# Padding the SBUF pools of a decoder layer so that what TensorE reads starts at multiples of 256 bytes

## The chip, the cores and the metric

One core of a Trainium2 chip runs one program. The metric is the device time of one execution in microseconds, less is better. Engines: TensorE (PE in the profile, its weight loads apart as PEld), VectorE (DVE), ScalarE (ACT), GpSimd (POOL) and SyncE (SP, which issues most DMAs). SBUF is the on-chip memory that all of them read; a tile takes the same bytes in each of 128 partitions. TensorE writes to PSUM.

## What is computed

A decoder layer on 512 tokens of 1,024 features, float32 in and out:

```python
h = rmsnorm(x, g_mix);  proj = h @ w_in
# a gated DeltaNet group (conv, l2norm, chunked delta rule) and a sparse-attention group
# (indexer, top-k of 128 keys, softmax with a position bias)
x = x + concat([o_dn, o_dsa]) @ w_out
qx = rmsnorm(x, g_xattn) @ w_xq;  kvx = rmsnorm(mem, g_mem) @ w_xkv   # 256 memory tokens
x = x + softmax_attention(qx, kvx) @ w_xo
hf = rmsnorm(x, g_ffn)
x = x + (silu(hf @ w_gate) * (hf @ w_up)) @ w_down                    # 2816 wide
return rmsnorm(x, g_final)
```

## The kernel before

Activations lie feature-major: a tile [128 features, 512 tokens] for each 128 features. For precision at speed, each large product is made of three: a float32 operand is split into a high part, rounded to float32r (the type that TensorE reads in one pass), and the low rest, also float32r. `split` (lines 128 to 130) does it, with a copy on ScalarE and a subtraction on VectorE, and `mm3` (lines 136 to 139) issues the three matmuls, the weights' part first and the activations' second in the call: the first is stationary, the second moving. In the profile's names the moving tile comes first: `ps<-XH,wh` streams XH over the stationary wh.

```python
def mm3(o, lh, ll, rh, rl, start, stop):
    pe.matmul(o, lh, rh, start=start, stop=False)
    pe.matmul(o, lh, rl, start=False, stop=False)
    pe.matmul(o, ll, rh, start=False, stop=stop)
```

`weights` (lines 143 to 157) loads 512 KB into wraw (one of three buffers, issued by SP), and splits it into wh and wl (two buffers each). `dense` (line 159) makes 8 times three matmuls of 512 columns with it. That is how the projections of the head (`project`), the output projections (`project_out`), the queries of the cross attention and the gate, up and down projections of the FFN (`gated`, line 1021, and the loop behind it) work. The keys of the cross attention have 256 columns. The values (lines 937 to 939), the gates of the DeltaNet group (496 to 498) and the last part of the down projection (1061 to 1063) are token-major: there the weights are moving and the activations stationary. The very last of these use wz, one large split tile, for 48 matmuls. At the start, x is multiplied with the 464 columns of w_in of the sparse-attention group (lines 280 to 282), from tiles wd, wdh and wdl of [128, 2, 464]. A few products are plain float32: the DeltaNet's own, the logits of half of the sparse heads, and the transposes, which multiply by an identity out of cst.

The order of each engine's instructions comes from the program's order and from a scheduler that the framework runs when the kernel is built. Where a tile lies is decided by pools: const, wp (weights) and tmp from the left end of the free part of SBUF, others behind them, and the pools called "right" from the right end downwards. A pool packs its tiles one behind the other, at multiples of 32 bytes. The free part begins at byte 16,512 and ends at 229,344. The const pool holds many small tiles (`small`, line 216: columns of statistics, 4 to 128 bytes), so what stands behind it begins wherever their sum ends.

Of the kernel before, what the change touches and what calls it, by code (L numbers as in the profile page):

```python
# [16 lines left out]
T = 512  # L17
# [10 lines left out]
# pairs of DSA heads whose logits are products over 128 partitions  # L28
# [3 lines left out]
_CONST_COLS = 6 * 128  # L32
# [33 lines left out]
def laid_out(a):  # L66
    """Inputs as the launch takes them: x feature-major, vectors gathered by partition or into one row."""
    par = []
    for name in PAR:
        v = np.asarray(a[name])  # L70
        par.append(np.tile(v.reshape(1, 64), (1, 2)) if name.startswith("kidx") else v.reshape(-1, 128))
    rows = [np.asarray(a[name]).reshape(-1) for name in ROW]
    r = {name: np.ascontiguousarray(a[name]) for name in _INS}
    r["xT"] = np.ascontiguousarray(np.asarray(a["x"])[0].T)
    r["w_ukT"] = np.ascontiguousarray(np.asarray(a["w_uk"])[0].transpose(2, 0, 1)).reshape(128, 512)
    r["w_uvT"] = np.ascontiguousarray(np.asarray(a["w_uv"])[0].transpose(1, 0, 2)).reshape(128, 512)
    r["params"] = np.ascontiguousarray(np.concatenate(par).T)
    r["rows"] = np.ascontiguousarray(np.concatenate(rows)).reshape(1, N_ROW)
    return r
# [3 lines left out]
def hybrid_block(ctx, tc, I, out):  # L83
# [3 lines left out]
    const = ctx.enter_context(tc.tile_pool(name="const", bufs=1))  # L87
    wp = ctx.enter_context(tc.tile_pool(name="wp", bufs=1))
# [77 lines left out]
    # ---------------------------------------------------------------- constants and parameters  # L166
# [15 lines left out]
    warm = const.tile([128, 128], FT, name="warm")  # L182
# [5 lines left out]
    prT = const.tile([128, N_PAR], FT, name="prT")  # L188
    act.dma_start(prT, I["params"])
    w_in = I["w_in"][0]  # L190
    wd = [xload.tile([128, 2, N_DSA], FT, name=f"wd{j}") for j in range(4)]
# [9 lines left out]
    cst = const.tile([128, 6, 128], FT, name="cst")  # L201
    ident, tri, ones = cst[:, 0, :], cst[:, 1, :], cst[:, 5, :]
    sp.dma_start(cst, I["consts"].rearrange("p (k c) -> p k c", c=128))
    brow = const.tile([128, N_ROW], FT, name="brow")
# [6 lines left out]
    mhalf = const.tile([128, 16], FT, name="mhalf")  # L211
# [4 lines left out]
    def small(n, dt=FT):  # L216
        n_small[0] += 1
        return const.tile([128, n], dt, name=f"sm{n_small[0]}")
# [6 lines left out]
    def row_of(cols):  # L225
        """[128 tokens, 4 tiles] -> [128, 512] with the same row on every partition."""
        q = ps()
        for t in range(NT):
            pe.matmul(q[:, t * 128:(t + 1) * 128], cols[:, t:t + 1].to_broadcast([128, 128]), ident,
                      start=True, stop=True)  # L230
        o = const.tile([128, T], FT, name=f"row{n_small[0]}", tag="row", bufs=1)
        act.activation(o, q, AF.Copy)
        return o

    class Stats:
        """Sum of squares of feature-major tiles, per token."""
# [21 lines left out]
    # ---------------------------------------------------------------- x, and the DSA columns token-major  # L258
# [3 lines left out]
    wdh, wdl = ([xload.tile([128, 2, N_DSA], FR, name=f"wd{x}{j}") for j in range(4)] for x in "hl")  # L262
# [31 lines left out]
    # norms of the small projections, and their transposes  # L294
# [43 lines left out]
    # ---------------------------------------------------------------- GDN projections of one head, feature-major  # L338
# [33 lines left out]
    # ---------------------------------------------------------------- indexer scores  # L372
# [4 lines left out]
    for pr_ in range(4):  # L377
        q = ps()
        ms = slice(pr_ * 128, (pr_ + 1) * 128)
        for k in range(2):  # L380
            mm3(q, wq[:, 0, k, ms], wq[:, 1, k, ms], cqh[k], cql[k], k == 0, k == 1)
        # [high part; low part] of a head's queries on 128 partitions meets the keys' high part in one product
        st = qst[pr_]
        ql = cv(dt=FR)
        for s, r in enumerate(HALF):
            act.activation(st[s][r], q[r], AF.Copy)
            dve.tensor_tensor(ql[r], q[r], f32(st[s][r]), op=OP.subtract)
            sp.dma_start(f32(st[s][HALF[1 - s]]), f32(ql[r]))
# [30 lines left out]
    # ---------------------------------------------------------------- decay and beta, columns (head, chunk)  # L419
# [24 lines left out]
    # decay between the tokens of a chunk, and from its start  # L444
# [14 lines left out]
    # ---------------------------------------------------------------- relative position bias  # L459
    rb = const.tile([32, 8], FT, name="rb")  # L460
# [5 lines left out]
    # minus the bias, so that a row's minimum is minus the maximum of its logits, and from the far bucket's on:  # L466
    # a softmax is the same for logits that are all moved by one number
# [7 lines left out]
    def topk():  # L475
        m8 = dsa.tile([128, 8], FT, name="m8")
        for it in range(16):
            for t in (3, 2, 1):
                dve.max(m8, score[t])  # L479
                dve.match_replace(score[t], m8, score[t], MARK)  # L480
            yield
        for t in (1, 2, 3):
            dve.tensor_scalar(score[t], score[t], MARK, -NEG, op0=OP.not_equal, op1=OP.mult)
        yield
# [25 lines left out]
    def latents():  # L510
        """Queries and keys of the DSA heads, in pairs; values token-major."""
        u = [gdn.tile([128, 512], FT, name=n, tag=f"zg{i}") for i, n in enumerate(("w_ukT", "w_uvT"))]
        sp.dma_start(u[0], I["w_ukT"])
        sp.dma_start(u[1], I["w_uvT"])
        for pr_ in range(4):
            ms = slice(pr_ * 128, (pr_ + 1) * 128)
            q = ps("mm")
            for k in range(2):
                mm3(q, wu[:, 0, k, ms], wu[:, 1, k, ms], cqh[k], cql[k], k == 0, k == 1)
            qd.append(dsa.tile([128, T], FT, name=f"qd{pr_}", tag=f"od{pr_}"))  # L520
            act.activation(qd[pr_], q, AF.Copy, scale=-0.125)
            q = ps("mm")
            pe.matmul(q, u[0][:, ms], ckvT, start=True, stop=True)
            kT.append(dsa.tile([128, T], FT, name=f"kT{pr_}", tag=f"ol{pr_}"))
            act.activation(kT[pr_], q, AF.Copy)
        for t in range(NT):
            q = ps("mm")
            pe.matmul(q, ckvT[:, t * 128:(t + 1) * 128], u[1], start=True, stop=True)
            vt.append(dsa.tile([128, 512], FT, name=f"vt{t}"))
            act.activation(vt[t], q, AF.Copy)  # L530

    # ---------------------------------------------------------------- DSA attention
    OD = []

    def attention():
# [5 lines left out]
        for pr_ in range(4):  # L541
# [8 lines left out]
            if pr_ in STACKED:  # L550
                # per head, [high part; low part] of the queries on 128 partitions, and the keys' high part twice
# [10 lines left out]
            for t in range(NT):  # L562
# [9 lines left out]
                for s in range(2):  # L572
# [16 lines left out]
                    # block (keys kb, queries t) at column 384 kb + 128 t  # L589
# [16 lines left out]
    # ---------------------------------------------------------------- gated delta rule  # L606
# [58 lines left out]
    def diagonal_blocks():  # L665
        """Inverse of the 16 x 16 diagonal blocks, one per partition."""
# [10 lines left out]
        # 4 x 4 blocks by substitution, then twice the size: X21 = X22 (- N21) X11  # L677
# [27 lines left out]
    def level(lev):  # L705
        """Inverse of twice the block size: X -= X C X, with C the blocks below the diagonal."""
# [17 lines left out]
    def last_level():  # L724
        """The same for the one pair of blocks that is left, rows 64: and columns :64 of C."""
# [20 lines left out]
    def recurrence():  # L746
        # q scale: sigma = 128^-1/2 (|q|^2 + eps)^-1/2
# [12 lines left out]
        for c in range(NT):  # L760
# [9 lines left out]
            if c:  # L770
                q = ps("g")
                heads(q, lambda h: (QK[h][:, 0, cs], S[:, h, :]))
                # one accumulation group for the four heads: only its first product clears the bank
# [80 lines left out]
    # ---------------------------------------------------------------- residual stream, feature-major  # L854
# [25 lines left out]
    # memory, normalised and feature-major  # L880
# [25 lines left out]
    # first the heads that are done first  # L906
# [4 lines left out]
    # ---------------------------------------------------------------- cross attention  # L911
# [31 lines left out]
    def probs(h):  # L943
        a_, b_ = (xa.tile([128, 2, T], FR, name=f"px{x}{h}", tag=f"px{x}", bufs=2) for x in "hl")
        PX[h] = a_, b_
        for t2 in range(2):
# [7 lines left out]
            c4 = tmp.tile([128, 8], FT, name=f"x4_{h}_{t2}", tag="x4", bufs=4)  # L954
# [58 lines left out]
    # ---------------------------------------------------------------- SwiGLU  # L1013
# [31 lines left out]
    # the last columns, with the residual stream and the rest of the layer token-major  # L1045
# [9 lines left out]
    for hf in range(2):  # L1055
# [14 lines left out]
        if hf:  # L1070
            # the last pieces as one, so that the tiles are done one after another
            raw, wh, wl = (ff.tile([128, 4, 512], d_, name=f"wz{i}") for i, d_ in enumerate((FT, FR, FR)))
            sp.dma_start(raw, I["w_down"][0, 18 * 128:, cols].rearrange("(k p) c -> p k c", p=128))
            split(wh, wl, raw)
            for t in range(NT):
                for k in range(4):
                    part(t, wh, wl, k, 2 + k)
# [17 lines left out]
    banks["pool"].release()  # L1095

# [19 lines left out]
```

## Time and profile before

| | |
|---|---|
| median of 3 runs | 875.5 us (872.02 to 876.1) |
| span of the profiled execution | 875.0 us |
| TensorE busy | 846.8 us (97%) |
| VectorE, ScalarE, GpSimd busy | 501.9, 368.1, 207.8 us |
| DMA | 87.00 MB, mean 99 GB/s |

The span runs from the first to the last instruction of one profiled execution; of that execution no other time is known, and the three runs beside it are other executions. Busy time of TensorE is the union of its matmuls, which overlap in a pipeline: the next one starts while the one before is still draining. What a matmul costs is therefore the distance between starts, not its duration.

### The profile page before, as it was taken

The page shows a single profiled execution, that of the slowest core. Times are in us where ns is not written, and L with a number is a line of the kernel's source. Part 1 is how long each engine was busy: PE and PEld are TensorE (multiplying, and loading weights), DVE is VectorE, ACT ScalarE, POOL GpSimd, SP SyncE. Part 2 cuts the span into 40 slices and gives each one's busy share as a digit, 9 for nine tenths or more (in the row PEclk, how much of TensorE's full clock was granted, in tenths as well). Part 3 has the DMA queues.
Part 4 walks back from the last instruction along what each step waited for, and adds up shares of the span by engine and source line. Part 5 has one row for each costly group of instructions (what it writes and reads, how often), then busy time and mean ns, then how long its engine had stood idle before and what let it go on. Part 6 is the DMA issues. An engine that isn't in the chain of part 4 may idle for free.

```text
span 875.0 us, 10849 instructions
## 1 busy us (share of the span) xinstructions
PE 846.8 (97%) x4058; PEld 680.2 (78%) x4058; DVE 501.9 (57%) x873; ACT 368.1 (42%) x723; POOL 207.8 (24%) x213
## 2 busy tenths in 40 slices
PE   9999969789999999999999999999999999999996
PEld 7876847678767889888887888888888888888885
DVE  8786759989777564464455444453344443345542
ACT  6573846435666543353434432221133222233332
POOL 5546835546321122000003221110011110001112
PEclk9998979999999999999999999999999999999999
DMA  8541355244022434243323533233333333323302
GB/s 282 144 101 47 42 124 137 66 109 97 19 55 84 158 97 145 81 137 101 97 67 98 167 97 97 84 90 106 88 90 96 97 97 97 96 81 88 97 24 97
DMA packets 136652, 87.00 MB, mean 99 GB/s; under 512 B 9688, under 2 KB 125592, under 8 KB 136600
## 3 DMA queue, kind: packets, MB, share of 16 engines
q1 hardware_dynamic: 135736, 84.69, 34.1%
q10 hardware_dynamic: 864, 1.62, 0.5%
q8 instruction: 32, 0.52, 0.2%
q14 instruction: 20, 0.16, 0.1%
HBM read 77.10 MB, written 7.09 MB: 96 GB/s over the span
## 4 chain that ended last, share of the span: by engine, by line
PE 82%; DMA 6%; DVE 6%; issue 2%; ACT 2%; POOL 1%; SPq 0%; POOLq 0%; ACTq 0%; DVEq 0%
PE ps L137 21%; PE ps L139 21%; PE ps L138 21%; DMA tb_d<-t2k 4%; PE ps L597 1%; PE ps L568 1%; PE ps L588 1%; PE ps L398 1%; PE ps L396 1%; PE ps L1061 1%; PE ps L1063 1%; PE ps L1062 1%; PE ps L766 1%; PE ps L937 1%; PE ps L939 1%
## 5 line engine op out<-in xcount | busy, mean ns | idle before, releaser
L129 ACT ACTIVATE wh<-wraw 128x1024 fp32r<-128x1024 f32 x120 | 127.2, 1061 | 319.6 <-PE ps L138 179.0
L137 PE MATMUL ps<-XH,wh 128*128 128x512 f32 x512 | 204.3, 399 | 0.0
L139 PE MATMUL ps<-XH,wl 128*128 128x512 f32 x512 | 203.7, 398 | 0.0
L138 PE MATMUL ps<-XL,wh 128*128 128x512 f32 x512 | 203.1, 397 | 0.0
L130 DVE TENSOR_TENSOR wl<-wraw,wh 128x1024 fp32r<-128x1024 f32 x108 | 153.7, 1424 | 67.6 <-ACT wh L129 67.2
L137 PEld LDWEIGHTS ps<-XH,wh 128*128 128x128 f32 x512 | 96.9, 189 | 22.6 <-ACT Dm L454 0.6
L138 PEld LDWEIGHTS ps<-XL,wh 128*128 128x128 f32 x512 | 96.8, 189 | 22.0 <-issue 0.2
L139 PEld LDWEIGHTS ps<-XH,wl 128*128 128x128 f32 x512 | 96.9, 189 | 21.6
L1032 POOL TENSOR_TENSOR t2k<-t2k,t2k 128x512 f32<-128x512 f32 x22 | 30.6, 1390 | 297.4 <-DVE t2k L1031 249.7
L247 POOL TENSOR_TENSOR acc<-acc,t2k 128x512 f32<-128x512 f32 x21 | 36.0, 1715 | 179.4 <-ACT t2k L246 179.1
L1031 DVE TENSOR_TENSOR t2k<-ps,row 128x512 f32<-128x512 f32 x22 | 15.2, 691 | 70.7 <-PE ps L139 70.7
L139 PE MATMUL ps<-HH,wl 128*128 128x512 f32 x128 | 50.7, 398 | 0.0
L137 PE MATMUL ps<-HH,wh 128*128 128x512 f32 x128 | 50.7, 396 | 0.0
L138 PE MATMUL ps<-HL,wh 128*128 128x512 f32 x128 | 50.2, 395 | 0.0
L1043 DVE TENSOR_TENSOR XR<-ps,XR 128x512 f32<-128x512 f32 x16 | 11.1, 692 | 54.2 <-PE ps L139 54.2
L1029 DVE TENSOR_TENSOR t2k<-ps,row 128x512 f32<-128x512 f32 x22 | 15.2, 692 | 37.7 <-PE ps L139 37.7
L130 POOL TENSOR_TENSOR wl<-wraw,wh 128x1024 fp32r<-128x1024 f32 x12 | 29.9, 2492 | 17.0 <-ACT wh L129 16.5
L873 DVE TENSOR_TENSOR XR<-ps,XR 128x512 f32<-128x512 f32 x16 | 11.0, 690 | 31.4 <-PE ps L139 31.4
L138 PEld LDWEIGHTS ps<-HL,wh 128*128 128x128 f32 x128 | 24.0, 188 | 5.8
L139 PEld LDWEIGHTS ps<-HH,wl 128*128 128x128 f32 x128 | 24.0, 188 | 5.8
L137 PEld LDWEIGHTS ps<-HH,wh 128*128 128x128 f32 x128 | 24.0, 188 | 5.5
L479 DVE MAX8 m<-masks 128x8 f32<-128x512 f32 (+2 forms) x48 | 26.6, 554 | 2.3 <-POOL masks L413 1.6
(396 smaller groups left out, 1669.5 us busy)
## 6 DMA issues: line engine op xcount, KB each, us to landing
wraw<-in_w_gate SPq DMA_DIRECT2D x22, 512.0 KB
wraw<-in_w_up SPq DMA_DIRECT2D x22, 512.0 KB, 3.9
wraw<-in_w_down SPq DMA_DIRECT2D x20, 512.0 KB, 3.9
wraw<-in_w_in SPq DMA_DIRECT2D x16, 512.0 KB, 4.2
wraw<-in_w_xkv SPq DMA_DIRECT2D x16, 512.0 KB, 3.8
wraw<-in_w_out SPq DMA_DIRECT2D x8, 512.0 KB, 4.1
wraw<-in_w_xq SPq DMA_DIRECT2D x8, 512.0 KB, 4.0
wraw<-in_w_xo SPq DMA_DIRECT2D x8, 512.0 KB, 3.9
```

The source lines that it names most:

```text
L129: act.activation(h, src, AF.Copy)
L130: (sub or dve).tensor_tensor(l, src, f32(h), op=OP.subtract)
L137: pe.matmul(o, lh, rh, start=start, stop=False)
L138: pe.matmul(o, lh, rl, start=False, stop=False)
L139: pe.matmul(o, ll, rh, start=False, stop=stop)
L247: pool.tensor_tensor(self.acc, self.acc, s_, op=OP.add)
L479: dve.max(m8, score[t])
L873: dve.tensor_tensor(XR[m], o, XR[m], op=OP.add)
L1029: dve.tensor_tensor(s1, og_, Rrow2, op=OP.mult)
L1031: dve.tensor_tensor(s2, ou_, Rrow2, op=OP.mult)
L1032: pool.tensor_tensor(s1, s1, s2, op=OP.mult)
L1043: dve.tensor_tensor(XR[m], o, XR[m], op=OP.add)
```

## The change

Every pool from the left is made to begin at a multiple of 256 bytes: a first tile fills the const pool up to the line, the sizes of its tiles are counted (`held` takes the place of `const.tile` throughout), and a last tile fills the pool's end. A tile called edge does the same at the right end. Inside the pools, tiles whose size isn't a multiple of 256 are widened: wd, wdh and wdl from 464 to 512 columns in memory (464 are still used), m8 from 8 to 64, and the little c4 tiles of the cross attention get 8 buffers instead of 4. cst becomes the first tile of const. Comments go, which shifts line numbers by up to 15.

```diff
-_CONST_COLS = 6 * 128
+LINE, FIRST, LAST = 256, 16512, 229344
...
     const = ctx.enter_context(tc.tile_pool(name="const", bufs=1))
+    n_const = [FIRST % LINE]
+    def held(shape, name, dt=FT, **kw):
+        if kw.get("tag") is None or kw["tag"] not in n_const:
+            n_const[0] += -(-int(np.prod(shape[1:])) * 4 // 32) * 32
+            n_const.append(kw.get("tag"))
+        return const.tile(list(shape), dt, name=name, **kw)
+    held((128, (LINE - FIRST % LINE) // 4), "head")
+    cst = held((128, 6, 128), "cst")
+    edge = ctx.enter_context(tc.tile_pool(name="edge", bufs=1, side="right"))
+    edge.tile([128, LAST % LINE // 4], FT, name="edge")
...
-    wd = [xload.tile([128, 2, N_DSA], FT, name=f"wd{j}") for j in range(4)]
+    wd = [xload.tile([128, 2, 512], FT, name=f"wd{j}")[:, :, :N_DSA] for j in range(4)]
...
-        return const.tile([128, n], dt, name=f"sm{n_small[0]}")
+        return held((128, n), f"sm{n_small[0]}", dt)
...
-        m8 = dsa.tile([128, 8], FT, name="m8")
+        m8 = dsa.tile([128, 64], FT, name="m8")[:, :8]
...
-            c4 = tmp.tile([128, 8], FT, name=f"x4_{h}_{t2}", tag="x4", bufs=4)
+            c4 = tmp.tile([128, 8], FT, name=f"x4_{h}_{t2}", tag="x4", bufs=8)
...
+    if n_const[0] % LINE:
+        const.tile([128, (LINE - n_const[0] % LINE) // 4], FT, name="tail")
```

The built programs tell where each operand starts. This is the table of places: the start's remainder modulo 256 bytes for the moving and the stationary tile of the float32r matmuls, before. In the changed program every entry is 0.

| matmuls | lines | columns | moving at | stationary at |
|---|---|---|---|---|
| 1,536 | 137 to 139, XH and XL with wh and wl | 512 | 64 | 192 |
| 48 | 137 to 139, cq with wq and wu | 512 | 64 | 192 |
| 384 | 137 to 139, HH and HL with wh and wl | 512 | 224 | 192 |
| 192 | 137 to 139, oxh and oxl with wh and wl | 512 | 224 | 192 |
| 192 | 496 to 498, 937 to 939, wh and wl with XH, XL, MH, ML | 512 | 192 | 64 |
| 96 | 1061 to 1063, wh and wl with HH and HL | 512 | 192 | 224 |
| 192 | 137 to 139, odh, odl, OGh, OGl with wh and wl | 512 | 192 | 192 |
| 48 | 137 to 139, pxh and pxl with Vh and Vl | 512 | 224 | 224 |
| 48 | 1061 to 1063, wz with HH and HL | 512 | 224 | 224 |
| 192 | 137 to 139, MH and ML with wh and wl | 256 | 64 | 192 |
| 96 | 137 to 139, KTh and KTl with qxh and qxl | 256 | 224 | 224 |
| 96 | 280 to 282, wdh and wdl with XH and XL | 464 | 32, 96, 160, 224 | 64 |
| 72 | 396, 398, 570, 571, stacked heads | 256 to 512 | 64, 192 | 192 |

Of 577 plain float32 matmuls, 575 have their moving tile at 0 after the change; of the stationary ones 541 do, the others are single columns of statistics, columns of U and the bias table. On every engine the built program has as many instructions as before, in the same order.

## Rows read from the trace of the kernel before

**Rows 1.** Head of the page; busy engines, and the granted clock in 40 slices
```profile
span 875.0 us, 10849 instructions
...
PE 846.8 (97%) x4058; PEld 680.2 (78%) x4058; DVE 501.9 (57%) x873; ACT 368.1 (42%) x723; POOL 207.8 (24%) x213
...
PEclk9998979999999999999999999999999999999999
```

**Rows 2.** The chain that ended last, shares of the span by engine
```profile
PE 82%; DMA 6%; DVE 6%; issue 2%; ACT 2%; POOL 1%; SPq 0%; POOLq 0%; ACTq 0%; DVEq 0%
```

**Rows 3.** Timeline of TensorE; start and duration in us, at 700 us
```profile
699.87 0.40 PE L137 MATMUL ps<-XH,wh 128*128 128x512 f32 x1
700.11 0.40 PE L138 MATMUL ps<-XL,wh 128*128 128x512 f32 x1
700.34 0.39 PE L139 MATMUL ps<-XH,wl 128*128 128x512 f32 x1
700.57 0.39 PE L137 MATMUL ps<-XH,wh 128*128 128x512 f32 x1
```

**Rows 4.** Stretches: us, TensorE busy (instructions), granted clock, DMA share, GB/s
```profile
630.16:719.15 88.99, 88.99 (x384) 1.00 0.33 95
585.36:629.92 44.56, 44.56 (x192) 1.00 0.33 95
857.01:867.69 10.68, 10.68 (x48) 1.00 0.20 76
331.36:336.99 5.63, 5.63 (x48) 1.00 0.33 96
16.17:17.02 0.85, 0.85 (x5) 1.00 1.05 407
67.67:70.23 2.56, 2.56 (x7) 0.50 0.00 0
0.00:240.00 240.00, 220.48 (x1076) 0.96 0.41 106
240.00:875.00 635.00, 626.29 (x2983) 1.00 0.33 97
```

**Rows 5.** Timeline of TensorE, plain float32 products between 140 and 144 us
```profile
140.75 1.02 PE L649 MATMUL ps<-QK 128*128 128x256 f32 x4
141.62 1.02 PE L528 MATMUL ps<-w_uvT,ckvT 128*128 128x512 f32 x2
142.47 1.03 PE L649 MATMUL ps<-QK 128*128 128x256 f32 x4
143.34 0.38 PE L624 MATMUL ps<-cst,QK 128*128 128x128 f32 x2
```

**Rows 6.** Groups, forms apart: busy us, mean ns of one, idle before
```profile
L137 PE MATMUL ps<-XH,wh 128*128 128x512 f32 x512 | 204.3, 399 | 0.0
...
L129 ACT ACTIVATE wh<-wraw 128x1024 fp32r<-128x1024 f32 x120 | 127.2, 1061 | 319.6 <-PE ps L138 179.0 <-issue 118.2 <-PE ps L1063 7.3
...
L137 PE MATMUL ps<-HH,wh 128*128 128x512 f32 x128 | 50.7, 396 | 0.0
...
L137 PE MATMUL ps<-OGh,wh 128*128 128x512 f32 x32 | 12.5, 389 | 0.0
...
L1061 PE MATMUL ps<-wz,HH 128*128 128x512 f32 x16 | 6.2, 390 | 0.0
```

More of the change, by code (lines that the diff above doesn't have):

```diff
@@ L180, in hybrid_block @@
     xt = [xload.tile([128, T], FT, name=f"xt{k}") for k in range(KD)]
-    warm = const.tile([128, 128], FT, name="warm")
+    warm = held((128, 128), "warm")
     dve.memset(warm, 0.0)
@@ L186, in hybrid_block @@
         pe.matmul(pw[:, :128], warm, warm, start=True, stop=True)
-    prT = const.tile([128, N_PAR], FT, name="prT")
+    prT = held((128, N_PAR), "prT")
     act.dma_start(prT, I["params"])
     w_in = I["w_in"][0]
-    wd = [xload.tile([128, 2, N_DSA], FT, name=f"wd{j}") for j in range(4)]
+    wd = [xload.tile([128, 2, 512], FT, name=f"wd{j}")[:, :, :N_DSA] for j in range(4)]
     def load_dsa(k0, kt):
@@ L200, in hybrid_block @@
             load_dsa(k, 1 if k < 2 else 2)
-    cst = const.tile([128, 6, 128], FT, name="cst")
     ident, tri, ones = cst[:, 0, :], cst[:, 1, :], cst[:, 5, :]
     sp.dma_start(cst, I["consts"].rearrange("p (k c) -> p k c", c=128))
-    brow = const.tile([128, N_ROW], FT, name="brow")
+    brow = held((128, N_ROW), "brow")
     sp.dma_start(brow, bass.AP(tensor=I["rows"].tensor, offset=I["rows"].offset, ap=[[0, 128], [1, N_ROW]]))
@@ L209, in par @@
         return prT[:, PAR[name] + k:PAR[name] + k + 1]
-    mhalf = const.tile([128, 16], FT, name="mhalf")
+    mhalf = held((128, 16), "mhalf")
     pool.memset(mhalf, -0.5)
@@ L230, in row_of @@
                       start=True, stop=True)
-        o = const.tile([128, T], FT, name=f"row{n_small[0]}", tag="row", bufs=1)
+        o = held((128, T), f"row{n_small[0]}", tag="row", bufs=1)
         act.activation(o, q, AF.Copy)
@@ L261, in hybrid_block @@
     stats = Stats()
-    wdh, wdl = ([xload.tile([128, 2, N_DSA], FR, name=f"wd{x}{j}") for j in range(4)] for x in "hl")
+    wdh, wdl = ([xload.tile([128, 2, 512], FR, name=f"wd{x}{j}")[:, :, :N_DSA] for j in range(4)] for x in "hl")
     for j in range(4):
@@ L457, in hybrid_block @@
         pool.tensor_tensor(Dm[:, h], Dm[:, h], tri[:, None, :].to_broadcast([128, NT, 128]), op=OP.mult)
-    rb = const.tile([32, 8], FT, name="rb")
+    rb = held((32, 8), "rb")
     sp.dma_start(rb, I["rel_bias"])
```

## The prediction, made before the changed kernel ran

> **What bounds the kernel now.** I read the head of the page first: the TensorE row is at 97% of the span, VectorE at 57%, ScalarE at 42%, and the granted clock stands at 9 tenths or more in all but two of the 40 slices [rows 1]. The chain that ended last is TensorE for 82% of the span, with 6% of DMA and 6% of VectorE [rows 2]. A busy TensorE need not be a TensorE at its best, so the next question is how far apart the matmuls start. The timeline shows steps of 0.23 and 0.24 us in the gate and up projections [rows 3]. The table of stretches gives them more finely. The instruction before reaches into each stretch, so a row has one start fewer than its count. From 630.16 to 719.15 us 383 matmuls of 512 columns start in 88.99 us, **232.35 ns each**; from 585.36 to 629.92 us 191 start in 44.56 us, **233.3 ns each** [rows 4]. The granted clock is 1.00 there, so the engine is at 2.4 GHz, and 512 columns alone are 213.3 ns. Each matmul costs 19 to 20 ns more than its columns.
>
> Three more rows tell something about these 19 ns. First, at the lower clock they are gone: six matmuls of the same kind start in 2.56 us at a granted clock of 0.50, 426.7 ns each, exactly 512 columns at 1.2 GHz [rows 4]. Second, plain float32 products, which pass each column at half the pace (two records for a product), hardly have them: eight records of 256 columns and two of 512 take 2.59 us, against 2.56 us by their columns, 3 ns a record [rows 5]. Third, the excess hardly grows with the columns: 47 matmuls of 256 columns in 5.63 us are 119.8 ns each, 13.1 over their 106.7; four of 464 columns in 0.85 us are 212.5 ns each, 19.2 over 193.3 [rows 4]. So it is a charge for each instruction, paid only when a new 4-byte column is read in every cycle at 2.4 GHz.
>
> Does the address matter for it? One stretch answers half of that. The last matmuls read wz against HH, both tiles at 224 modulo 256 in the table of places, and 47 of them start in 10.68 us, **227.2 ns each** [rows 4]. The same HH tiles met wh and wl (224 against 192) at 233.3 ns. In the groups, products whose two tiles lie at one offset have the shorter durations, 389 ns for OGh with wh (192 and 192) and 390 for wz with HH, against 399 for XH with wh (64 and 192) and 396 for HH with wh [rows 6]. Offset 192 stands in the faster and in the slower group, so it isn't that offset as such: equal offsets are 5 to 6 ns better than unequal ones. What the trace doesn't hold is any such product with a tile at 0: every fast one lies off the 256-byte line, and there 13.9 of the 19 to 20 ns remain.
>
> **The change, part by part.** All 3,192 float32r products get both tiles at 0 modulo 256. Of these, 2,736 have 512 columns. With unequal offsets today are 1,584 at 232.35 ns (XH or XL with wh or wl, 512 in each of three lines, and the 48 with cq) and 864 that I price at 233.3 ns (384 of HH and HL, 192 of oxh and oxl, 192 with wh or wl moving at L496 to L498 and L937 to L939, 96 at L1061 to L1063). With equal offsets are 288 at 227.2 ns. Further 288 have 256 columns, 96 have 464, and the 72 at L396 to L398, L570 and L571 I leave out.
>
> What one costs when both tiles start on the line is the unknown. From below it is bounded by the columns with the 3 ns that the float32 records show: 216.3, 109.7 and 196.3 ns. From above, if equal offsets are all that counts, by 227.2 ns, and if the address doesn't matter, by today's steps. A loss isn't excluded: the worst step in the rows is 0.24 us, and equal starts could make it the rule.
>
> I take the lower bound. The excess of equal offsets is a fixed charge that vanishes wherever the reading has slack (the lower clock, the half pace); a start off the line, which costs one more fetch that can't be made up when there is no slack, would look like this, and an inherent cost of changing the weights would rather be seen in the float32 records too. Then: 1,584 by (232.35 - 216.3) is 25.4 us; 864 by 17.0 is 14.7; 288 by 10.9 is 3.1; 288 of 256 columns by 10.1 is 2.9; 96 of 464 columns by 16.2 is 1.6. **Together 47.7 us of TensorE.**
>
> How much of that is on the path? After 240 us TensorE is busy for 626.3 of 635 us, so a nanosecond there is a nanosecond of the end. Before, it is busy for 220.5 of 240 us [rows 4] and others set the pace in part. In that part lie 336 of the 1,584, 96 of the 864 and all of the 464-column ones: 5.4 + 1.6 + 1.6 = 8.6 us, of which I count half. 47.7 - 4.3 = 43.4 us, and 875.0 - 43.4 is 831.6 us of span. The median of the runs is 0.5 us above this span, so 832.
>
> [...]
>
> What else has to keep up: 24 matmuls use one 512 KB weight tile; at 216.3 ns that is 5.2 us instead of 5.6. ScalarE needs 1.06 us for its copy, and in the dense stretch DMA stands at 0.33 of its time [rows 4, 6], so a twelfth more in rate fits. The other edits I cost at nothing. The split of the x weights runs over 2x464 columns with a gap instead of 928, at the start, under the loads of x. The four more buffers for c4 in the cross attention can only remove a wait. Padding costs bytes, not instructions: on each engine as many instructions stand as before, in one order, so no queue is moved past.
>
> **The rivals.**
> *Only equal offsets count.* Then 227.2 ns is the floor: 1,584 by 5.15 is 8.2 us and 864 by 6.1 is 5.3, together 13.4; less half of the 2.3 us that lie before 240 us, 12.3, so **863**. For it: 227.2 ns is seen at both 192 and 224, with 64 and 32 bytes before the next line, and nothing shows that 0 is different. Against: it leaves 14 ns that the half-pace records don't have.
> *Addresses don't count at all* and the wz stretch is fast for another reason (both of its tiles stand still, no weight buffer turns over): **875.5**. Against it stands OGh, fast at equal offsets with turning buffers.
> [...]
> *Equal starts collide.* If moving and stationary reads that both start at 0 hit the same part of the memory at once, in the dense loop of L137 to L139, the worst step of 0.24 us becomes every step: 1,584 by 7.65, 864 by 6.7 and 288 by 12.8 ns are 21.6 us, **897**. It decides from a mean step of 512 columns above 232.1 ns, the mean of the three groups today. Against: the equal offsets of today are the fast ones.
>
> **How the numbers follow.** Full effect 0.50, equal offsets only 0.25, something between these two 0.06, no effect 0.13, collision 0.06. The likeliest gives 832. The range runs from 826 (the whole 47.7 us and a little of hidden waits) to 865 (the second case with a runs' spread of a few us to spare): it holds the first three cases, 0.81. About 0.5%, 4.4 us, is what a measurement of this kernel can tell from no change, so faster is 0.81, the same 0.13, slower 0.06.
>
> **What would show it.** Right: in the gate and up projections steps of about 216 ns, so that 384 matmuls take 83 us instead of 89; in the keys' projection 110 ns for 256 columns; steps at the clock of 0.50 unchanged at 426.7 ns; TensorE still at 97%. If equal offsets are all, the dense steps and those of wz are both 227. The sum is wrong, though the step is right, if 216 ns show and the chain has new pieces of DMA or of wraw's split between the tiles: then the weights have become the bound. And the whole is wrong if wz and HH, both moved from 224 to 0, still stand at 227 ns.

## The result and the profile after

| | before | changed |
|---|---|---|
| runs beside the prediction | 873.76 us median of 4 | 865.31 us median of 4 (861.88 to 867.8) |
| ratio, 95% interval | | 0.9882 (0.9855 to 0.9908) |
| span of the profiled execution | 875.0 us | 861.3 us |
| TensorE busy | 846.8 us | 836.3 us |

The change makes the kernel faster, by 1.2%. The forecast was 832 us; 865.31 lies just beyond the range's end of 865, and beside the second case (863). A second timing of the same kernel, told below, gave 0.9822 (0.9784 to 0.9861). The ratios leave out executions in a slower state, over 1.5% above the fastest of the same kernel: two of the six of that second timing are such.

The stretches of the changed kernel that answer to [rows 4], in the same columns, the first four with the same work:

```profile
621.77:708.58 86.81, 86.81 (x384) 1.00 0.34 97
578.25:621.54 43.29, 43.29 (x192) 1.00 0.34 96
843.44:854.10 10.66, 10.66 (x49) 1.00 0.20 76
328.62:334.25 5.63, 5.63 (x48) 1.00 0.34 95
...
0.00:240.00 240.00, 223.62 (x1090) 0.95 0.41 107
```

The dense stretch has 383 steps of 226.7 ns instead of 232.35, and that of HH 191 of 226.7 instead of 233.3. The stretch of wz, whose tiles went from 224 to 0 modulo 256, has 47 steps of 226.8, where they were 227.2 (a count may take in an instruction more at either edge). The 256 columns take 119.8 ns as before, though their starts were 64 and 192: at this width unequal starts had cost nothing. So in long rows the matmuls of 512 columns now cost what those with equal starts cost already, and none costs less. The groups (columns as in [rows 6]) say the same in durations, 393 for 399 and 390 for 396, and no change for OGh:

```profile
L151 PE MATMUL ps<-XH,wh 128*128 128x512 f32 x512 | 201.3, 393 | 0.0
...
L151 PE MATMUL ps<-HH,wh 128*128 128x512 f32 x128 | 49.9, 390 | 0.0
...
L151 PE MATMUL ps<-OGh,wh 128*128 128x512 f32 x32 | 12.5, 389 | 0.0
```

Equal starts alone don't give 226.7 ns at once. The products of pxh and pxl stood at 224 and 224 before and stand at 0 and 0 now; they come right behind float32 transposes, and ten of their steps take 2.31 us, 231 ns each. The 24 steps of XH and XL that follow, with the same equal starts, take 226.7 ns:

```profile
392.98:395.29 2.31, 2.31 (x11) 1.00 0.00 0
395.29:400.73 5.44, 5.44 (x25) 1.00 0.34 99
```

Counted over the whole trace at the full clock, the first nine steps of 512 columns behind other work take 224 to 236 ns, some 230 on average; from the tenth on they take 226.7. Before the change both parts stood at 232. Short rows of matmuls thus gain little: the 96 of the gates (L496 to L498 before) still take some 231 ns a step at the full clock, where they took 233.

Where the time came from is seen when both spans are cut at the same pieces of work: the first matmul of the mixing layer's output projection, the second half of the gate and up projections, the first matmul with wz. Before, then after:

```profile
0.00:285.86 285.86, 265.27 (x1362) 0.96 0.39 102
285.86:630.16 344.30, 343.59 (x1660) 1.00 0.36 107
630.16:857.01 226.85, 226.85 (x993) 1.00 0.29 84
857.01:875.00 17.99, 11.07 (x49) 0.94 0.32 118
```

```profile
0.00:283.12 283.12, 265.66 (x1362) 0.96 0.38 103
283.12:621.77 338.65, 337.93 (x1659) 1.00 0.37 108
621.77:843.44 221.67, 221.67 (x993) 1.00 0.30 86
843.44:861.30 17.86, 11.04 (x49) 0.96 0.31 118
```

The two middle pieces, in which TensorE is never idle for long, give 5.65 and 5.18 us, the first 2.74, the last 0.13. Together they are the 13.7 us of the span. In the first piece TensorE's busy time didn't fall (265.27 and 265.66 us): its 2.74 us are idle time.

### The profile page after: what moved, and what is told of

It reads as the page before. It is cut to its first block, busy times and chain, and to the rows that moved or that the text cites. A ratio compares the mean times of both kernels' runs of the same rounds, so it can differ in the third digit from the quotient of the medians.

```text
span 861.3 us, 10848 instructions
## 1 busy us (share of the span) xinstructions
PE 836.3 (97%) x4058; PEld 680.3 (79%) x4058; DVE 503.0 (58%) x873; ACT 368.5 (43%) x723; POOL 206.7 (24%) x213
## 4 chain that ended last, share of the span: by engine, by line
PE 82%; DMA 7%; DVE 6%; ACT 2%; issue 1%; SPq 0%; POOL 0%; POOLq 0%; ACTq 0%; DVEq 0%
PE ps L151 21%; PE ps L152 21%; PE ps L153 21%; DMA tb_d<-t2k 4%; PE ps L610 1%; PE ps L581 1%; PE ps L411 1%; PE ps L601 1%; PE ps L409 1%; PE ps L1076 1%; PE ps L1075 1%; PE ps L1074 1%; PE ps L779 1%; PE ps L950 1%; PE ps L951 1%
## 5 line engine op out<-in xcount | busy, mean ns | idle before, releaser
L143 ACT ACTIVATE wh<-wraw 128x1024 fp32r<-128x1024 f32 x120 | 127.2, 1061 | 310.2 <-PE ps L152 173.1
L151 PE MATMUL ps<-XH,wh 128*128 128x512 f32 x512 | 201.3, 393 | 0.0
L153 PE MATMUL ps<-XH,wl 128*128 128x512 f32 x512 | 200.5, 392 | 0.0
L152 PE MATMUL ps<-XL,wh 128*128 128x512 f32 x512 | 200.1, 391 | 0.0
```

The source lines that it names most:

```text
L143: act.activation(h, src, AF.Copy)
```

## The experiments

I had two theories left. **A**: what counts is the difference between the starts of the moving and of the stationary tile, modulo 256 bytes; the line itself doesn't matter. **B**: a start off the line of 256 bytes costs by itself, and something else holds the rest.

**Everything at 64.** The padding stays, but moves each pool 64 bytes off the line:

```diff
-LINE, FIRST, LAST = 256, 16512, 229344
+LINE, FIRST, LAST, AT = 256, 16512, 229344, 64
...
-    held((128, (LINE - FIRST % LINE) // 4), "head")
+    held((128, (LINE + AT - FIRST % LINE) // 4), "head")
...
-    edge.tile([128, LAST % LINE // 4], FT, name="edge")
+    edge.tile([128, (LAST - AT) % LINE // 4], FT, name="edge")
...
-    if n_const[0] % LINE:
-        const.tile([128, (LINE - n_const[0] % LINE) // 4], FT, name="tail")
+    if (n_const[0] - AT) % LINE:
+        const.tile([128, (AT - n_const[0]) % LINE // 4], FT, name="tail")
```

> All pools are moved by 64 bytes, so that every float32r operand starts at 64 modulo 256, moving and stationary alike; nothing else changes. Theory A (only the difference between the two starts counts): dense steps stay at 227 ns and the time at that of the changed kernel, about 865 us. Theory B (a start off the 256-byte line costs by itself): dense steps over 227 ns, up to 232, and 870 us or more.

Measured: 861.24 us, ratio to the kernel before 0.9834 (0.9808 to 0.986). The dense stretch, in the columns above:

```profile
619.96:706.77 86.81, 86.81 (x385) 1.00 0.34 97
```

That is 226.7 ns a step with no operand on a line. B falls.

**The weights at 128.** The same padding, and 128 bytes more between const and wp, taken back by a first tile of 128 bytes in tmp:

```diff
+    tmp.tile([128, 32], FT, name="gap")
...
-    if n_const[0] % LINE:
-        const.tile([128, (LINE - n_const[0] % LINE) // 4], FT, name="tail")
+    const.tile([128, ((LINE - n_const[0]) % LINE + 128) // 4], FT, name="tail")
```

> Only the pool of the weights is moved by 128 bytes against the changed kernel: wh and wl at 128, nearly everything else still at 0, all on 128-byte multiples. Theory A (the difference counts, modulo 256): 2,304 matmuls of 512 columns with 0 against 128 and 288 with 128 against 0 go back to 232 ns, about 13 us more, 875 us. Theory B (each operand's own place on a line of 128 bytes or less counts): no change, about 865 us.

Measured: 875.63 us, ratio 1.0009 (0.9986 to 1.0031). The gain is gone, in the place that A names: dense steps of 232.4 ns, while those of wz, still equal, stay at 227.

```profile
628.00:717.00 89.00, 89.00 (x384) 1.00 0.33 94
583.39:627.77 44.38, 44.38 (x193) 1.00 0.33 95
854.65:865.32 10.67, 10.67 (x49) 1.00 0.20 76
```

**Matmuls alone.** A kernel of stretches of 48 matmuls, each reading 8 tiles in turn, without work on another engine:

```diff
...
+            pe.matmul(o[0:m, 0:n], S[:, os_ + (k % 8) * 128:os_ + (k % 8) * 128 + m],
+                      M[:, om + (k % 8) * 512:om + (k % 8) * 512 + n], start=k == 0, stop=k == count - 1)
```

> Matmuls alone, with no other engine at work, 48 in a stretch; nothing of the layer is computed, the output is a copy of mem. Theory A (difference of the starts): 227 ns at a difference of 0 and of 256 bytes and with both at 64 or both at 128; about 232 to 233 ns at 32, 64, 128 and 224 bytes, whichever tile is moved. Rival (other engines' traffic makes the 5 ns): 227 ns or less everywhere. For the 11 ns that are left over 216: if reading the weights takes cycles from the moving stream, 64 and 32 stationary columns make it smaller, 221 and 219 ns; if it is a fixed cost of float32r, they don't, and bfloat16 alone is at 216 ns.

The stretches from the first to the last start, 47 steps each; in this order both at 0, moving at 32, at 128, at 256, stationary at 128, both at 64, both at 128, then 64 and 32 stationary columns with both at 0, and 256 columns with both at 0:

```profile
20.20:30.85 10.65, 10.65 (x48) 1.00 0.01 2
...
53.52:64.48 10.96, 10.96 (x49) 1.00 0.01 1
...
86.92:97.89 10.97, 10.97 (x48) 1.00 0.01 1
...
131.74:142.40 10.66, 10.66 (x48) 1.00 0.00 0
142.64:153.56 10.92, 10.92 (x48) 1.00 0.01 2
153.79:164.48 10.69, 10.69 (x48) 1.00 0.00 0
164.71:175.41 10.70, 10.70 (x49) 1.00 0.00 0
175.64:186.44 10.80, 10.80 (x48) 1.00 0.01 2
197.78:208.66 10.88, 10.88 (x48) 1.00 0.01 2
219.96:225.59 5.63, 5.63 (x49) 1.00 0.00 0
```

The first seven are 226.6, 233.2, 233.4, 226.8, 232.3, 227.4 and 227.7 ns: A, with a period of 256 bytes, and without any other engine at work, so their traffic isn't the cause. Both at 64 and both at 128 are 0.8 and 1.1 ns above both at 0. Of the differences of 4, 16, 64 and 224 bytes (11.09, 10.88, 10.77 and 10.96 us) 64 cost least (229.1 ns, under the 232 that were expected) and 4 most (236.0 ns); 16 and 224 stand at 231.5 and 233.2. Narrower weights make it no better, 229.8 and 231.5 ns, so the 11 ns that are left aren't paid by the column of weights.

A holds for 512 moving and 128 stationary columns, and not at the other widths tried. In order: 64 and 32 stationary columns and 256 moving columns, all three with the moving tile at 128, then 384 columns with both at 0 and with the moving tile at 128:

```profile
186.68:197.55 10.87, 10.87 (x49) 1.00 0.00 0
208.89:219.73 10.84, 10.84 (x49) 1.00 0.00 0
225.71:231.29 5.58, 5.58 (x49) 1.00 0.01 3
...
231.41:239.58 8.17, 8.17 (x49) 1.00 0.00 0
239.75:248.03 8.28, 8.28 (x48) 1.00 0.00 0
```

With narrow weights unequal starts are at 231.3 and 230.6 ns, no worse than equal ones by more than 1.5; with 256 columns they are at 118.7 against 119.8, and with 384 at 176.2 against 173.8. Forty steps of bfloat16 take 8.63 us, 215.8 ns, both at a difference of 0 and of 128 bytes (the first few are left out, since a record is missing there):

```profile
249.73:258.36 8.63, 8.63 (x41) 1.00 0.00 0
260.09:268.72 8.63, 8.63 (x41) 1.00 0.00 0
```

**One edit of the change.** In the built program the left pools were apart by 128 bytes because of tmp alone. So:

```diff
-            c4 = tmp.tile([128, 8], FT, name=f"x4_{h}_{t2}", tag="x4", bufs=4)
+            c4 = tmp.tile([128, 8], FT, name=f"x4_{h}_{t2}", tag="x4", bufs=8)
```

> The kernel before with one edit of the change alone: 8 buffers instead of 4 for the c4 tiles of the cross attention, 128 bytes more in the pool tmp. By the built program this moves everything that lies left behind tmp by 128 bytes, to 192 modulo 256, where wh and wl already lie: 1,776 of the 2,448 unequal matmuls of 512 columns become equal, none at a multiple of 256. HH, HL, oxh and oxl stay at 224 against 192. Theory A (the difference of the starts, modulo 256, is all): steps of 227 ns for XH and XL, 233 for HH; 1,584 by 5.15 and 192 by 6.1 ns are 9.3 us less, with part of the early ones hidden 8 to 9 us, a ratio of 0.990. If the buffers themselves matter, the steps stay at 232 ns and only waits in the cross attention go.

Measured: 870.33 us, ratio 0.9936 (0.9907 to 0.9965), a smaller gain than expected, with 0.990 just outside; the steps are as expected, 226.8 ns for XH and 233.4 for HH.

```profile
629.35:716.20 86.85, 86.85 (x384) 1.00 0.34 97
584.55:629.12 44.57, 44.57 (x193) 1.00 0.33 95
...
0.00:200.00 200.00, 182.60 (x787) 0.91 0.45 115
```

In the first 200 us this execution was granted a clock of 0.91, that of the changed kernel 0.94 (its row stands below). TensorE got less far there, 787 instructions against 819. Over the whole span the runs behind this ratio were granted 0.977 to 0.986, those of the kernel before beside it 0.979 to 0.990, most of them 0.985 or more; the one at 0.986 took 865.36 us, 0.988 of the 875.45 before. The clock may thus be what is missing, but one run doesn't show it.

```profile
0.00:200.00 200.00, 184.56 (x819) 0.94 0.44 116
```

**Three edits.** The same with two more:

```diff
+    edge = ctx.enter_context(tc.tile_pool(name="edge", bufs=1, side="right"))
+    edge.tile([128, 8], FT, name="edge")
...
-        m8 = dsa.tile([128, 8], FT, name="m8")
+        m8 = dsa.tile([128, 64], FT, name="m8")[:, :8]
```

> The kernel before with 8 buffers for c4, a tile of 32 bytes at the right end, and m8 widened to 64 columns. By the built program all float32r operands of 512, 256 and 384 columns then start at 192 modulo 256, moving and stationary alike, none on a multiple of 256. Theory A: as fast as the whole change, ratio 0.983 to 0.988, dense steps of 227 ns everywhere. Theory B (the line of 256 bytes): slower than the whole change.

Measured: 865.13 us, ratio 0.9879 (0.9842 to 0.9917), with XH and HH at 226.7 ns:

```profile
623.35:710.16 86.81, 86.81 (x385) 1.00 0.33 97
579.83:623.12 43.29, 43.29 (x193) 1.00 0.34 98
```

These three edits do what the whole padding does; the first tile, the counting in `held`, the widened wd and the tail add nothing that these runs could tell.

**What the last 11 ns are.** Two more kernels of matmuls alone. In the first both starts move on together; then one column is repeated:

```diff
+            a = (k * step) % 64
...
+        pe.matmul(o, st[:, k % 8 * 128:k % 8 * 128 + 128], mv[:, k % 8 * 512:k % 8 * 512 + 1].to_broadcast([128, 512]),
...
```

> Matmuls alone as before, equal starts of moving and stationary tile in each, but both starts move on by some bytes from one matmul to the next; then one column, or one weight column, read again and again. Nothing of the layer is computed. If the 11 ns over 216 that equal starts leave are a wait until the next start comes round on a grid of 128 or 256 bytes, some of these advances (32 bytes, or its complement) give about 217 ns and others more than 227. If they are a fixed cost of a float32r matmul, all equal advances give 227 ns or more. A repeated column of the moving tile at 216 ns would say that the 11 ns belong to the reading of the moving tile; a repeated weight column, that they belong to the reading of the weights.

In order: no advance, 32 and 128 bytes of advance, one moving column repeated, one weight column repeated.

```profile
22.52:33.17 10.65, 10.65 (x48) 1.00 0.01 2
66.82:77.82 11.00, 11.00 (x48) 1.00 0.00 0
111.30:122.03 10.73, 10.73 (x48) 1.00 0.01 2
178.30:188.45 10.15, 10.15 (x49) 1.00 0.00 0
188.66:199.56 10.90, 10.90 (x49) 1.00 0.00 0
```

No advance is best: 226.6 ns against 234.0 and 228.3. Equal starts are thus not quite enough, they must also stay at the same place from one matmul to the next. The trace shows why that may be so: the weights of a matmul are loaded while the one before it runs (before the change, the load for L139 at 771.05 us takes 0.19 us beside the matmul of L138, which starts at 771.05). Whether a moving tile's own weights count or the next ones, no run here separates. A repeated moving column costs 216.0 ns, a repeated weight column 231.9. The 11 ns go when the moving tile brings nothing new, and not when the weights don't. In the kernel before there is a weight load for each matmul (4,058 of each [rows 1]); what the load itself has to do with the 11 ns isn't shown.

```diff
+                m = m[:, 0:512 // how[1]].unsqueeze(2).to_broadcast([128, 512 // how[1], how[1]])
...
+                m = m.rearrange("p (b a c) -> p a b c", a=how[0], c=how[1])
```

> Matmuls alone, all starts at 0 modulo 256, 48 in a stretch; nothing of the layer is computed. The moving tile's 512 columns are read in other ways: each column twice or four times, a part of them again and again, or pieces of 1 to 64 columns alternately left out and read afterwards. If the 11 ns are paid for the amount of new bytes that the moving tile brings, columns read twice or four times at once give 216 ns, and so do parts that are repeated only if the bytes are kept; if they are paid for each matmul with more than one place to read, all of these stay at 227 ns. If they come from an order that meets the weights' reading badly, one of the orders with pieces apart is nearer to 216 ns, and a kernel could use it.

In order: as ever, each column twice, half of the columns twice over, pieces of 4 columns apart, pieces of 64 columns (256 bytes) apart.

```profile
22.80:33.45 10.65, 10.65 (x48) 1.00 0.01 2
33.68:43.82 10.14, 10.14 (x48) 1.00 0.00 0
54.40:65.10 10.70, 10.70 (x49) 1.00 0.01 2
109.56:120.54 10.98, 10.98 (x48) 1.00 0.00 0
143.64:154.33 10.69, 10.69 (x48) 1.00 0.00 0
```

At half the pace of new columns the 11 ns are gone (215.7 ns); at full pace they stay, whether the bytes were read before or not (227.7 for the half read twice over, 226.6 as ever). Pieces of 4 columns are slower (233.6 ns), pieces of 256 bytes hardly (227.4). None of these orders came out below 226 ns at full pace, so there was no version to build on one.

**The change and everything at 64, side by side**, the two kernels as above, timed again on one chip.

> The changed kernel as it is, timed beside the next one on the same chip. Theory A: ratio to the kernel before of 0.983 to 0.99, and equal to that of the kernel with everything at 64 within 0.5%.

> Everything at 64 modulo 256, timed beside the changed kernel. Theory A: the same time as the changed kernel within 0.5%, in spite of the earlier ratios of 0.9834 here and 0.9882 there, which come from stretches at the lower clock in the first 200 us that differ from run to run. If 64 is better than 0 as such: again some 0.5% faster.

Measured: 0.9822 (0.9784 to 0.9861) for the change, just under the 0.983 that was expected, and 0.9861 (0.9833 to 0.989) for everything at 64. Earlier the order was the other way round; the intervals overlap, so nothing is shown for 0 over 64, nor against it.

## Why the prediction was wrong

The direction and the place were right: the dense steps shrink, and TensorE stays at 97%. The prediction's own sign of being wrong is what came: wz and HH, both moved from 224 to 0, still stand at 227 ns.

The step that failed is "I take the lower bound": 216.3 ns for a matmul whose tiles both start on the line. The runs showed 226.7 ns, which is the bound from above for the case that equal offsets are all that counts. The reason that I gave, that a start off the line costs one more fetch when there is no slack, is wrong: with everything at 64 the steps are the same, 226.7 ns, and no run shows such a fetch. The fact behind it was right, and the reading orders confirm it: the 11 ns are gone when each column is read twice (215.7 ns) or one is repeated (216.0). But at the full pace of new columns every start that was tried pays them, and my argument that they would then show in the float32 records forgot that these run at half of it (0.22 us for a record of 256 columns [rows 5]).

By that one step each term was oversized: 1,584 matmuls gained 5.7 ns by the dense stretch instead of 16.05, 864 gained 6.6 by that of HH instead of 17.0, the 288 equal ones and the 288 of 256 columns gained nothing or half a nanosecond instead of 10, and the 96 of 464 columns 1 to 2 (some 211 to 210 ns at the full clock) instead of 16.2. I also read one charge where there are two: about 13 ns over the columns at any start, and some 6 more for unequal starts at 512 columns. The 256 columns, at 64 against 192, had only the first.

The rows give the 213.3 ns for 512 columns, on which the 216.3 stand, only as an estimate: half of the 426.7 ns of a step at the granted clock of 0.50 [rows 4]. They have the granted share of the clock and no GHz; the prediction's 2.4 is 512 columns in those 213.3 ns. In the changed kernel, at equal starts, six steps of L509 to L511 at that clock take 2.56 us again, 426.7 ns each, so the difference of the starts costs nothing there:

```profile
167.18:169.74 2.56, 2.56 (x7) 0.50 0.27 104
```

At a granted clock of 1.00 the shortest stretch of 512 columns told here is that of the columns read twice, 215.7 ns a step.

The case "only equal offsets count" was the right one. The trace's witness for it was in the text: 227.2 ns at 224, and durations as short at 192. A charge that was the same with 64 and with 32 bytes to the next line should have outweighed a mechanism that no row showed. What I left out of the groups are pxh and pxl, at equal offsets and yet at 396 to 408 ns; they are the short rows told above.

That its 863 us lies so near is in part luck. 1,584 by 5.7 and 864 by 6.6 ns would be 9.0 + 5.7 = 14.7 us, but TensorE's busy time fell by 10.5. Two estimates from the traces explain most of the rest: some 530 uneven steps at 3.5 ns are 1.9 us, and TensorE was busy at the granted clock of 0.50 for 15 us before and for 20 after, which is 2.5 us of work less. The other 3.2 us of the span are idle time of TensorE, 28.2 us before and 25.0 after; the same waits stand in it, mostly before 240 us, 21.2 and 18.1 us in all. They aren't shown to come from the change: with the weights at 128, where the dense steps gained nothing, the idle time was 23.7 us.

The rival by which addresses don't count falls with the weights at 128: 232.4 ns a dense step at a difference of 128 bytes, 226.7 at none. The matmuls alone agree: 32 and 128 bytes cost 5 to 7 ns, and 256 cost nothing. The collision is refuted too: with everything at 0 the dense steps are 226.7 ns, and not 240. Steps of 216 ns were met by bfloat16 (215.8) and by columns read twice or repeated (215.7 and 216.0), and by no float32r stream here in which every column differs from the one before (226.6 at best).

## What to carry to other kernels

Where float32r matmuls of 512 columns bound a kernel, look at the steps between their starts; if they are near 233 ns and not 227, compare the starts of moving and stationary tiles modulo 256 bytes in the built program. Making them equal takes a few bytes in the pools between them; a multiple of 256 isn't needed. Expect it to pay in rows of many such matmuls, not in rows of fewer than ten between other work (some 230 ns after, 232 before), and not at 256 columns (119.8 ns before and after). Before a forecast takes a floor that no row shows, look for the rows that already have the property in question, and price from them.

## What the runs showed of the hardware

Unexpected were three things. First, a float32r matmul costs about 13 ns over its columns even at equal starts: 226.7 ns for 512, 119.8 for 256, where the columns alone are an estimated 213.3 and 106.7 (from the 426.7 ns of 512 columns at a granted clock of 0.50). At a granted clock of 1.00 that charge was there in every stretch whose moving tile brought a new 4-byte column each time, with other engines at work (226.7 ns) or without (226.6); with each column read twice 2.4 ns of it are left (215.7 ns).

Second, the start of the weights against that of the moving tile counts, though they share no data. With 512 moving and 128 stationary columns a difference of 4, 16, 32, 128 or 224 bytes costs 5 to 9 ns (231.5 to 236.0 against 226.6), one of 64 bytes 2.5 (229.1), and one of 256 nothing (226.8). With 384 columns 128 bytes cost 2 ns (176.2 against 173.8), with 256 columns nothing (118.7 against 119.8), and with 64 or 32 stationary columns equal starts bring 1.5 ns or none (229.8 against 231.3, 231.5 against 230.6).

Third, equal starts work only in a row: behind other work the first nine or ten steps are uneven, 230 ns on average in the changed kernel, and then they stand at 226.7. Unequal starts didn't get there in any of these stretches of 47 steps (229.1 ns at best). Why a difference of 256 bytes counts like none, and what in the memory meets there, no run here shows.
